# A decoder layer on one core: the output gate's projection woven into the cached-token attention instead of the mLSTM, and the sequences' states loaded ahead of their scores

## The chip, the cores and the metric

The kernel runs on one core of a Trainium2 chip. The metric is the device time of one execution in microseconds (us). The kernel before took 1005.29 us (median of 3 runs, 1005.04 to 1005.99). Engines are called PE (TensorE, with PEld for its weight loads), DVE (VectorE), ACT (ScalarE), POOL (GpSimd) and SP (SyncE, which here only issues DMAs).

## The reference

One layer of a hybrid decoder, for a prompt of 512 tokens and, beside it, 8 sequences with 4 new tokens each. The mixer has two heads groups side by side, an mLSTM and a differential attention (DA), both fed by the same normalised rows `h`:

```python
h = rms_norm(x, g_mix_pre)
z = h @ w_in
q, k, v, o = mLSTM columns of z          # 4 heads x 128 each
h_ml, C_new, n_new, m_new = mlstm_chunkwise(q, k, v, i_pre, logf, ml_C, ml_n, ml_m)
h_ml = rms_norm(h_ml, g_ml_head) * sigmoid(o)
dq, dk, dv = DA columns of z             # rotated
a = attend(dq, dk, dv, lam)              # prompt: causal; sequences: cache of 256 tokens + own 4
h_da = rms_norm(a, g_da_head) * (1 - lam_init)
x = x + rms_norm(concat(h_ml, h_da) @ w_out, g_mix_post)
x = x + rms_norm(cross attention into 256 memory tokens, g_mem_post)
x = x + rms_norm(conv_ffn(...), g_ffn_post)
```

For the 8 sequences the mLSTM starts from a given state: a matrix `C` of 128 x 128 for each sequence and head (32 matrices, 64 KB each), which is read, used for the output, updated and written back.

## The kernel before

All tokens are held as 5 row blocks: four of 128 prompt rows and one of the 32 rows of the sequences. Weights pass through a pool `W` of 4 slots (`wp`); each weight tile is loaded by SP, split on ACT (L142) and DVE (L143) into a high and a low part, and multiplied in three passes, so that a product of fp32 accuracy comes out of reduced-precision matmuls. `gemmA` makes row-major products, `gemmB` (L452) transposed ones; a `gemmB` step is one 128-column weight tile: 8 x 3 x 2 = 48 matmuls, half of them 256 and half 288 columns wide.

`F` is a queue of filler work: generators of projections, from which `F.run(n)` takes pieces worth about n us and emits them at that place of the program. The final order of each engine is made by a scheduler that keeps the dependences and moves ready work about. In the program's order the stretch that matters here is:

- the prompt's mLSTM, a pipeline over the 4 prompt blocks (`ml_own`, `ml_state`, `ml_rows`), with the DA projections as filler. The last filler is the output gate's projection `o`: `gemmB(hT, [ev_T(soT, h) ...])`, 4 steps, 192 matmuls, into `soT` (L617);
- the sequences' mLSTM scores (L788 to L927): scores, key weights `kS`, the normaliser `n` (in from HBM as `nrow`, out as `nrow`);
- the sequences' states, called the state stage below. `mls_load` brings the four matrices of one head and four sequences as a tile `Cs` (256 KB). `mls_update` reads them into the output (`mlsi`, L949: 16 matmuls for each group of four sequences), makes the update (`vz` on POOL, L936; `mlus` on PE, L952), adds it on DVE (L954, four instructions for each tile) and writes the tile back (L956). There are 8 tiles, two groups of 4 heads; the loads of the second group are issued as the first is worked off. All of these tiles come from a pool `T2` of 8 buffers;
- the cached-token attention, called the cache stage below: for each of the 8 sequences `dk_turn` transposes 256 cached keys (`tpk`, L1158, 8 transposes a sequence) and `dk_scores` makes the scores (`ssc`, L1164). Woven between them is the prompt's DA (`sda`, L1179 and L1180; `tpa`, L1195; `oda`, L1205). `out_gate` (sigmoid on ACT, L987; scale on POOL, L988; transposes `mlt`, L995) is put in from its fourth step on. The product with the cached values (`ops`, L1247) follows.

PE works its instructions in the order in which they stand, and so does SP with its DMAs: what waits holds up everything behind it.

Of the kernel before, what the change touches and what calls it, by code (L numbers as in the profile page):

```python
# [15 lines left out]
P = 128  # L16
# [6 lines left out]
H = 4  # L23
# [50 lines left out]
def kernel(ctx: ExitStack, tc: tile.TileContext, I, O):  # L74
# [23 lines left out]
    def S(shape, dt, name):  # L98
        return sp.tile(list(shape), dt, name=name, tag="S")
# [4 lines left out]
    def T2(shape, name, dt=F32):  # L104
        return t2p.tile(list(shape), dt, name=name, tag="T2")
# [4 lines left out]
    def at(name="at"):  # L110
        return psa.tile([P, 512], F32, name=name, tag="at")

    def mmp(name="mm"):
        return psm.tile([P, 512], F32, name=name, tag="mm")
# [8 lines left out]
    def v2(t, b):  # L123
        return t.rearrange("p (a b) -> p a b", b=b)
# [10 lines left out]
    dma = nc.sync.dma_start  # L135

    def f32(ap):
        return ap.bitcast(F32)
# [6 lines left out]
    def rows(b):  # L145
        return (b * P, P) if b < 4 else (SEQ, NS)
# [4 lines left out]
    def con(n, p=P):  # L151
        o, w = CONST_COLS[n]
        return cpk[:p, o:o + w]
# [173 lines left out]
    allb = [0, 1, 2, 3, 4]  # L327

    class Fill:
# [8 lines left out]
        def run(self, amount=1e9):  # L338
            while amount > 0 and self.q:
                try:  # L340
                    amount -= next(self.q[0])
                except StopIteration:
                    self.q.pop(0)

    F = Fill()
# [5 lines left out]
    def pipe(n, *stages):  # L351

        for t in range(n + len(stages) - 1):
            for s in reversed(range(len(stages))):
                if 0 <= t - s < n:
                    stages[s](t - s)
            yield

    def sample_mm(ps, xs, w, start, stop):


        for kk, x in enumerate(xs):
            n = x.shape[0]
            for e in range(2):
                g = NS * (2 * kk + e)
                mm(ps[g:g + NS, :256], lhsT=x, rhs=w[:n, kk, 256 * e:256 * e + 256], start=start, stop=stop)  # L366
# [7 lines left out]
    def gemmA(xt, nk, blocks, evac, block_major=False, before=None, mid=None, late=False):  # L374


        ps = {}

        def one(b, k, s):
            if b == 4:  # L380
                if k % 2 == 0:
                    sample_mm(ps[b], [xt.sam(k), xt.sam(k + 1)], s[1], k == 0, k == nk - 2)
                return
            s, kk = s[0], k % 2
            c0, n = rows(b)
            mm(ps[b], lhsT=xt.hi(k, c0, c0 + n), rhs=s[:, 0, kk, :], start=(k == 0), stop=False)  # L386
            mm(ps[b], lhsT=xt.hi(k, c0, c0 + n), rhs=s[:, 1, kk, :], start=False, stop=False)  # L387
            mm(ps[b], lhsT=xt.lo(k, c0, c0 + n), rhs=s[:, 0, kk, :], start=False, stop=(k == nk - 1))  # L388

        if block_major:  # L390
            slots = [W.get() for _ in range((nk + 1) // 2)]
            for b in blocks:
                if before:
                    before(b)
                ps[b] = mmp()
                for k in range(nk):
                    if k == MIDK and mid:
                        mid()
                    one(b, k, slots[k // 2])
                    if b == blocks[-1] and k % 2 == 1:  # L400
                        W.free()
                evac(b, ps[b])
                yield 5.1
        else:
            for b in blocks:
                ps[b] = mmp()
            behind = []
            for k in range(nk):
                if k % 2 == 0:
                    s = W.get()  # L410
                    if 4 in blocks:
                        behind.append((k, s))
                        if not late:
                            one(4, *behind.pop(0))
                for b in blocks:
                    if b < 4:
                        one(b, k, s)
                if k % 2 == 1:
                    if len(behind) > 1:
                        one(4, *behind.pop(0))  # L420
                    if not late or k > 1:
                        W.free()
                yield sum(0.64 if b < 4 else 0.43 for b in blocks)
            for k, s in behind:
                one(4, k, s)
                W.free()
            for b in blocks:
                evac(b, ps[b])
            yield 0

    def gemmB(xt, evacs, half_first=False):

        if half_first:
            slots = [W.get() for _ in evacs]
            for i, (c0, c1) in enumerate(HALF):
                for s, ev in zip(slots, evacs):
                    ps = mmp()[:, :c1 - c0]
                    for k in range(8):
                        for j, (l, x) in enumerate(((0, xt.hi), (0, xt.lo), (1, xt.hi))):
                            mm(ps, lhsT=s[:, l, k, :], rhs=x(k, c0, c1), start=(k == 0 and j == 0), stop=(k == 7 and j == 2))  # L440
                    if i == 1:
                        W.free()
                    ev(i, c0, c1, ps)
                    yield 2.6
            return
        for ev in evacs:
            s = W.get()
            ps = [mmp()[:, :c1 - c0] for c0, c1 in HALF]
            for k in range(8):
                for j, (l, x) in enumerate(((0, xt.hi), (0, xt.lo), (1, xt.hi))):  # L450
                    for i, (c0, c1) in enumerate(HALF):
                        mm(ps[i], lhsT=s[:, l, k, :], rhs=x(k, c0, c1), start=(k == 0 and j == 0), stop=(k == 7 and j == 2))  # L452
                if k % 2 == 1 and k < 7:
                    yield 1.36
            W.free()
            for i, (c0, c1) in enumerate(HALF):
                ev(i, c0, c1, ps[i])
            yield 1.36
# [79 lines left out]
    hT = XT("hT")  # L538
# [76 lines left out]
    def ev_T(dst, h):  # L615
        def ev(i, c0, c1, ps):
            nc.scalar.copy(out=dst[:, h, c0:c1], in_=ps)  # L617
        return ev
# [147 lines left out]
    def ev_dv(b, ps):  # L766
# [4 lines left out]
        else:  # L771
# [1 line left out]
            dma(out=O["s_dv"][0].rearrange("b t h d -> (b t) (h d)"), in_=dvS)  # L773

    soT = S([P, H, ROWS], F32, "soT")
    F.add(gemmA(hT, 8, allb, ev_dk), gemmA(hT, 8, allb, ev_dq), gemmA(hT, 8, allb, ev_dv),
          gemmB(hT, [ev_T(soT, h) for h in range(H)]))


    def ml_scores(b):  # L780

        c0, n = rows(b)

        eb = T2([P, H, n], "mlE", F32R)
        GTT(out=eb, in0=f32(E2[:, c0:c0 + n]).unsqueeze(1).broadcast_to([P, H, n]),
            in1=hsel.unsqueeze(2).broadcast_to([P, H, n]), op=MUL)
        dv = at("mld")[:, :H * n].rearrange("p (h n) -> p h n", n=n)
        mm(dv[:n], lhsT=ones_r[:, :n], rhs=eb, start=True, stop=False)  # L788
        mm(dv[:n], lhsT=identb[:n, :n], rhs=(maskTb if b < 4 else maskSb).unsqueeze(1).broadcast_to([n, H, n]),
           start=False, stop=True)  # L790
        dm = T2([n, H, n], "mlD")
        for h in range(H):
            ACT(out=dm[:, h, :], in_=dv[:n, h, :], func=AF.Exp, bias=gt4[:n, b, 0, h:h + 1])
        sv = v2(at("mls"), P)[:, :, :n]
        for h in range(H):
            mm(sv[:n, h, :], lhsT=kT[:, h, c0:c0 + n], rhs=qT[:, h, c0:c0 + n], start=True, stop=True)
        VTT(out=dm, in0=sv[:n], in1=dm, op=MUL)
        return dm
# [17 lines left out]
    mlh, Cs, dms, wks = {}, {}, {}, {}  # L816
# [65 lines left out]
    dma(out=O["p_ml_n"][0, 0], in_=nrow)  # L882


    sm_t = ml_scores(4)
    pk = at("mlks")
    for h in range(H):
# [39 lines left out]
    dma(out=O["s_ml_n"][0].rearrange("b h d -> (b h) d"), in_=nrow1)  # L927

    pi = at("mlsi")
    csts, vzs = {}, {}  # L930

    def mls_values(i):

        g, h = i // H, i % H
        vzs[i] = T2([P, 4, P], "vz", F32R)
        GTT(out=vzs[i], in0=f32(vS[:, h, :]).unsqueeze(1).broadcast_to([P, 4, P]),  # L936
            in1=con("selX")[:, 4 * g:4 * g + 4].unsqueeze(2).broadcast_to([P, 4, P]), op=MUL)

    def mls_load(g, h):
        csts[g, h] = T2([P, 4, P], "Cs")  # L940
        dma(out=csts[g, h], in_=I["state_ml_C"][0, 4 * g:4 * g + 4, h].rearrange("b d e -> d b e"))

    def mls_update(i):
        g, h = i // H, i % H
# [13 lines left out]
            mls_load(1, h)  # L958
        F.run(2.5)

    for h in range(H):
        mls_load(0, h)
    run(pipe(2 * H, mls_values, mls_update))
    pn = at("mlsn")
    for h in range(H):
# [248 lines left out]
    STT(out=cv, in0=con("cB"), scalar=nlam, in1=con("cA"), op0=MUL, op1=ADD)  # L1214

    W.nslots = 2
    prompt = pipe(4 * H, da_soft, lambda i: None, da_turn, da_av, da_end)
    sall = S([P, NB, 260], F32, "das")
    nm, su = small(NB, "snm"), small(NB, "ssu")
    for t, _ in enumerate(pipe(NB, dk_load, dk_turn, dk_scores)):  # L1220
        if t == 3:
            F.add(out_gate())
        F.run(2.5)
        next(prompt)
        F.run(2.5)
    aw, az = sample_softmax(sall, su, cv, con("selD"), "da")
    F.run(4)
    pz = Z("pz")[:, :NS]
# [554 lines left out]
```

## Time and profile before

| | |
|---|---|
| median of 3 runs | 1005.29 us |
| the profiled execution's own time | 1005.6 us |
| its span, first to last instruction | 1003.8 us |
| mean granted PE clock | 0.986 |
| PE busy | 975.0 us |
| DVE, ACT, POOL busy | 601.9, 388.4, 195.4 us |

The profile is of one execution. "Busy" of PE counts a matmul from its start to its modelled end; matmuls overlap, so PE may be busy without being at its peak. A row of the timeline gives the start in us from the span's beginning, the time that the merged instructions took together, the engine, the line of the code, the operation, what it writes and reads, how many instructions were merged (one matmul on plain fp32 counts twice), and in brackets the idle time before it with what ended it. A row of a table by windows gives, for each engine, the busy time in that window, then the granted PE clock (1.00 is full speed) and the share of time in which the DMA engines were busy.

### The profile page before, as it was taken

To read this page: it belongs to the slowest core of one execution; us is meant where nothing else is said; L and a number is where in the kernel's file an instruction comes from. 1 tells how busy PE (TensorE), PEld (TensorE's weight loads), DVE (VectorE), ACT (ScalarE), POOL (GpSimd) and SP (SyncE) were. 2 spreads that over 40 slices of the span, in tenths; PEclk is the share of its full clock that TensorE was granted. 3 is DMA by queue.
4 is the path that set the end of the run, shared out by engine and by line. 5 is a ranking of instruction groups with operands and counts; after the bars stand their busy time and mean duration, and the time that the engine had idled before them with its cause. 6 is when DMAs were issued, how large, how long until landed. Compare 5 with 4: busy or idle time off the path is not lost.

```text
span 1003.8 us, 17048 instructions
## 1 busy us (share of the span) xinstructions
PE 975.0 (97%) x6615; PEld 813.2 (81%) x6615; DVE 601.9 (60%) x1129; ACT 388.4 (39%) x746; POOL 195.4 (19%) x389
## 2 busy tenths in 40 slices
PE   8999999999799999999999999999999999999994
PEld 5899777889555778998757789979987997997983
DVE  5735324643686357634653587836857685675677
ACT  5654313334376348633442444242222222222232
POOL 6510000112332124400000264301101010110115
PEclk9999999999799999999999999999999999999998
DMA  8950224152534167764851673052142314214113
GB/s 276 302 156 20 65 84 129 43 182 60 175 115 145 40 210 255 252 206 157 325 199 42 194 236 106 26 146 86 45 116 75 96 46 126 87 44 135 34 47 110
DMA packets 120401, 130.26 MB, mean 130 GB/s; under 512 B 8423, under 2 KB 85832, under 8 KB 120320
## 3 DMA queue, kind: packets, MB, share of 16 engines
q1 hardware_dynamic: 114136, 125.69, 40.6%
q10 hardware_dynamic: 6184, 3.48, 1.2%
q8 instruction: 52, 0.85, 0.3%
q14 instruction: 29, 0.24, 0.1%
HBM read 112.22 MB, written 16.93 MB: 129 GB/s over the span
## 4 chain that ended last, share of the span: by engine, by line
PE 87%; DVE 5%; DMA 4%; issue 2%; ACT 2%; POOL 1%; ACTq 0%; SPq 0%; DVEq 0%; POOLq 0%
PE mm L452 30%; PE mm L440 7%; PE mm L386 6%; PE mm L388 6%; PE mm L387 6%; PE mm L1626 4%; PE mm L1628 4%; PE mm L1627 4%; PE mm L366 3%; PE sda L1179 2%; PE tpk L1384 1%; PE sca L1335 1%; PE cpo L1365 1%; PE ssc L1394 1%; PE oda L1205 1%
## 5 line engine op out<-in xcount | busy, mean ns | idle before, releaser
L142 ACT CAST wslot<-wst 128x1024 fp32r<-128x1024 f32 (+1 forms) x127 | 131.1, 1036 | 278.8 <-issue 81.2
L452 PE MATMUL mm<-fT,wslot 128*128 128x256 f32 (+1 forms) x1872 | 235.7, 288 | 0.0
L452 PEld LDWEIGHTS mm<-fT,wslot 128*128 128x128 f32 x1872 | 234.7, 188 | 0.7 <-issue 0.4
L143 DVE TENSOR_TENSOR wslot<-wst,wslot 128x1024 fp32r<-128x1024 f32 (+1 forms) x127 | 154.0, 1215 | 109.7 <-ACT wslot L142 109.7
L1626 PE MATMUL mm<-wslot,act 128*128 128x512 f32 (+1 forms) x176 | 70.7, 409 | 0.0
L1627 PE MATMUL mm<-wslot,act 128*128 128x512 f32 (+1 forms) x176 | 69.5, 395 | 0.0
L1628 PE MATMUL mm<-wslot,act 128*128 128x512 f32 (+1 forms) x176 | 69.0, 397 | 0.0
L1533 POOL COPY cvo<-u 128x2 f32<-128x2 f32 x43 | 16.1, 375 | 222.8 <-DVE u L1531 222.8
L386 PE MATMUL mm<-wslot,hT 128*128 128x512 f32 x128 | 51.9, 408 | 0.0
L452 PE MATMUL mm<-hT,wslot 128*128 128x288 f32 (+1 forms) x384 | 51.4, 290 | 0.0
L387 PE MATMUL mm<-wslot,hT 128*128 128x512 f32 x128 | 51.2, 400 | 0.0
L388 PE MATMUL mm<-wslot,hT 128*128 128x512 f32 x128 | 50.7, 397 | 0.0
L452 PEld LDWEIGHTS mm<-hT,wslot 128*128 128x128 f32 x384 | 48.9, 188 | 0.9 <-issue 0.8
L1626 PEld LDWEIGHTS mm<-wslot,act 128*128 128x128 f32 (+1 forms) x176 | 33.1, 189 | 17.7 <-issue 8.6
L1528 DVE TENSOR_TENSOR u<-mm,rsb 128x256 f32<-128x256 f32 x43 | 18.1, 423 | 44.2 <-PE mm L452 43.3
L1628 PEld LDWEIGHTS mm<-wslot,act 128*128 128x128 f32 (+1 forms) x176 | 33.0, 188 | 7.5
L1627 PEld LDWEIGHTS mm<-wslot,act 128*128 128x128 f32 (+1 forms) x176 | 33.1, 188 | 6.5
L1545 ACT ACTIVATE c<-c 128x560 f32<-128x560 f32 x21 | 14.1, 672 | 57.3 <-DVE c L1539 57.2
L1539 DVE SCALAR_TENSOR_TENSOR c<-u,cvT,c 128x560 f32<-128x560 f32 x43 | 34.3, 798 | 0.8
L1538 DVE SCALAR_TENSOR_TENSOR c<-u,cvT,c 128x560 f32<-128x560 f32 x43 | 34.1, 794 | 0.1
L1639 DVE TENSOR_TENSOR yp<-mm,yp 128x512 f32<-128x512 f32 x40 | 27.3, 689 | 9.5 <-PE mm L1628 9.4
L386 PEld LDWEIGHTS mm<-wslot,hT 128*128 128x128 f32 x128 | 24.0, 188 | 10.3 <-issue 5.8
(458 smaller groups left out, 1885.8 us busy)
## 6 DMA issues: line engine op xcount, KB each, us to landing
wst<-in_w_up_dram SPq DMA_DIRECT2D x42, 512.0 KB
wst<-in_w_in_dram SPq DMA_DIRECT2D x28, 512.0 KB
wst<-in_w_down_dram SPq DMA_DIRECT2D x20, 512.0 KB
wst<-in_cache_mem_k_dram SPq DMA_DIRECT2D x16, 512.0 KB
vt<-in_cache_mem_v_dram SPq DMA_DIRECT2D x8, 1024.0 KB
wst<-in_w_mk_dram SPq DMA_DIRECT2D x8, 512.0 KB
xb<-in_x_prompt_dram SPq DMA_DIRECT2D x8, 512.0 KB
wst<-in_cache_dk_dram SPq DMA_DIRECT2D x16, 256.0 KB
```

The source lines that it names most:

```text
L142: nc.scalar.copy(out=hi, in_=src)
L143: (eng or nc.vector).tensor_tensor(out=lo, in0=src, in1=f32(hi), op=SUB)
L386: mm(ps[b], lhsT=xt.hi(k, c0, c0 + n), rhs=s[:, 0, kk, :], start=(k == 0), stop=False)
L387: mm(ps[b], lhsT=xt.hi(k, c0, c0 + n), rhs=s[:, 1, kk, :], start=False, stop=False)
L388: mm(ps[b], lhsT=xt.lo(k, c0, c0 + n), rhs=s[:, 0, kk, :], start=False, stop=(k == nk - 1))
L440: mm(ps, lhsT=s[:, l, k, :], rhs=x(k, c0, c1), start=(k == 0 and j == 0), stop=(k == 7 and j == 2))
L452: mm(ps[i], lhsT=s[:, l, k, :], rhs=x(k, c0, c1), start=(k == 0 and j == 0), stop=(k == 7 and j == 2))
L1538: STT(out=c, in0=u[:, 1:EXT - 1], scalar=w[1], in1=c, op0=MUL, op1=ADD)
L1539: STT(out=c, in0=u[:, 0:EXT - 2], scalar=w[0], in1=c, op0=MUL, op1=ADD)
L1626: mm(ps, lhsT=t[:, 0, c0:c0 + P], rhs=s[:n, 0, i % 2, :], start=st, stop=False)
L1627: mm(ps, lhsT=t[:, 0, c0:c0 + P], rhs=s[:n, 1, i % 2, :], start=False, stop=False)
L1628: mm(ps, lhsT=t[:, 1, c0:c0 + P], rhs=s[:n, 0, i % 2, :], start=False, stop=en)
```

## The change

Three things are moved; no computation is added or left out.

1. The output gate's projection is no longer filler of the mLSTM. It is put into the filler queue just before the cache stage.
2. In the cache stage each step takes two pieces of about 1 us from the filler queue in place of two of about 2.5 us. `out_gate` still joins the queue at the fourth step, now behind the projection.
3. The loads of the first four state tiles are issued before the sequences' scores instead of after them.

```diff
     soT = S([P, H, ROWS], F32, "soT")
-    F.add(gemmA(hT, 8, allb, ev_dk), gemmA(hT, 8, allb, ev_dq), gemmA(hT, 8, allb, ev_dv),
-          gemmB(hT, [ev_T(soT, h) for h in range(H)]))
+    F.add(gemmA(hT, 8, allb, ev_dk), gemmA(hT, 8, allb, ev_dq), gemmA(hT, 8, allb, ev_dv))
...
+    csts, vzs = {}, {}
+
+    def mls_load(g, h):
+        csts[g, h] = T2([P, 4, P], "Cs")
+        dma(out=csts[g, h], in_=I["state_ml_C"][0, 4 * g:4 * g + 4, h].rearrange("b d e -> d b e"))
+
+    for h in range(H):
+        mls_load(0, h)
     sm_t = ml_scores(4)
...
     pi = at("mlsi")
-    csts, vzs = {}, {}
-
     def mls_values(i):
...
-    def mls_load(g, h):
-        csts[g, h] = T2([P, 4, P], "Cs")
-        dma(out=csts[g, h], in_=I["state_ml_C"][0, 4 * g:4 * g + 4, h].rearrange("b d e -> d b e"))
...
-    for h in range(H):
-        mls_load(0, h)
     run(pipe(2 * H, mls_values, mls_update))
...
     W.nslots = 2
+    F.run()
+    F.add(gemmB(hT, [ev_T(soT, h) for h in range(H)]))
     prompt = pipe(4 * H, da_soft, lambda i: None, da_turn, da_av, da_end)
     sall = S([P, NB, 260], F32, "das")
     nm, su = small(NB, "snm"), small(NB, "ssu")
     for t, _ in enumerate(pipe(NB, dk_load, dk_turn, dk_scores)):
         if t == 3:
             F.add(out_gate())
-        F.run(2.5)
+        F.run(1)
         next(prompt)
-        F.run(2.5)
+        F.run(1)
```

What the scheduler made of it is seen in three places. The first is SP's queue around the state tiles. `Cs<-in_state_ml_C` is the load of a tile, `out<-Cs` the write of an updated one, `nrow` the normaliser's rows. Before:

```order
L882 DMA out_dram<-nrow 4x128
L900 DMA nrow_2292<-in_state_ml_n_dram 32x128
L941 DMA Cs<-in_state_ml_C_dram 128x4x128
L927 DMA out_dram<-nrow_2321 32x128
L941 DMA Cs<-in_state_ml_C_dram 128x4x128 x5
L956 DMA out_dram<-Cs 128x4x128 x2
L941 DMA Cs<-in_state_ml_C_dram 128x4x128 x2
L956 DMA out_dram<-Cs 128x4x128 x5
```

After (line numbers move with the edit: L888 is the load, L957 the write, L934 the second `nrow` out):

```order
L888 DMA Cs<-in_state_ml_C_dram 128x4x128 x2
L881 DMA out_dram<-nrow 4x128
L888 DMA Cs<-in_state_ml_C_dram 128x4x128 x2
L907 DMA nrow_2182<-in_state_ml_n_dram 32x128
L888 DMA Cs<-in_state_ml_C_dram 128x4x128
L934 DMA out_dram<-nrow_2211 32x128
L888 DMA Cs<-in_state_ml_C_dram 128x4x128
L957 DMA out_dram<-Cs 128x4x128
L888 DMA Cs<-in_state_ml_C_dram 128x4x128
L957 DMA out_dram<-Cs 128x4x128 x2
L888 DMA Cs<-in_state_ml_C_dram 128x4x128
L957 DMA out_dram<-Cs 128x4x128 x4
```

Four loads now stand ahead of the `nrow` load. The sixth load stands behind the second `nrow` write, the seventh behind the first tile's write and the eighth behind the second tile's write; in the built program each of these three waits for the end of that write, whose buffer it takes over. Before, six loads stood ahead of every tile's write, and only the eighth waited for one.

The second place is PE in the state stage (`mlsi` reads the states, `mlus` makes an update). Before, a piece from its beginning:

```order
L949 MATMUL mlsi<-Cs,qzm 32x128
L452 MATMUL mm<-hT_255,wslot 128x288
L452 MATMUL mm<-hT_256,wslot 128x256
L452 MATMUL mm<-hT_256,wslot 128x288
L952 MATMUL mlus<-vz,kS 128x512
L452 MATMUL mm<-hT_255,wslot 128x256
L949 MATMUL mlsi<-Cs,qzm 32x128 x13
```

After, the whole stage with the first rows of the cache stage:

```order
L950 MATMUL mlsi<-Cs,qzm 32x128 x16
L953 MATMUL mlus<-vz,kS 128x512
L950 MATMUL mlsi<-Cs,qzm 32x128
L953 MATMUL mlus<-vz,kS 128x512
L950 MATMUL mlsi<-Cs,qzm 32x128
L953 MATMUL mlus<-vz,kS 128x512 x2
L950 MATMUL mlsi<-Cs,qzm 32x128
L953 MATMUL mlus<-vz,kS 128x512
L950 MATMUL mlsi<-Cs,qzm 32x128 x13
L953 MATMUL mlus<-vz,kS 128x512 x3
L965 MATMUL mlsn<-tb,mlD 32x128 x4
L1157 MATMUL tpk<-cpk,wst 128x128 x16
```

No `L452` stands in this stage any more. Of the projection's 192 matmuls the first step's 48 stay ahead of the sequences' scores, among the last rows of the prompt's mLSTM, together with 4 `sda` pairs of the DA that stood in the state stage before. The third place is PE in the cache stage. Before:

```order
L1180 MATMUL sda<-cb 128x128
L1158 MATMUL tpk<-cpk,wst 128x128 x8
L1164 MATMUL ssc<-kT,qz 32x260 x4
L995 MATMUL mlt<-cpk,mlh 128x128 x4
L1205 MATMUL oda<-dvN,aT 128x128
L1195 MATMUL tpa<-cpk,pda 128x128
```

After:

```order
L1179 MATMUL sda<-cb 128x128
L1163 MATMUL ssc<-kT,qz 32x260 x4
L1157 MATMUL tpk<-cpk,wst 128x128 x2
L452 MATMUL mm<-hT_255,wslot 128x256
L452 MATMUL mm<-hT_255,wslot 128x288
L452 MATMUL mm<-hT_256,wslot 128x256
L452 MATMUL mm<-hT_256,wslot 128x288
```

The other 144 matmuls of the projection stand here, in runs of 2 to 19 between the attention's groups, and the 17 `mlt` transposes have moved to the stage's end. Behind the cache stage PE's order is the same but for a few rows.

## The prediction

> **What bounds the kernel now.** I read the page's first and fourth parts, then a table by windows around the change, then the timelines and the chain of waits there.
>
> ```profile
> PE 975.0 (97%) x6615; PEld 813.2 (81%) x6615; DVE 601.9 (60%) x1129; ACT 388.4 (39%) x746; POOL 195.4 (19%) x389
> ...
> PE 87%; DVE 5%; DMA 4%; issue 2%; ACT 2%; POOL 1%; ACTq 0%; SPq 0%; DVEq 0%; POOLq 0%
> ```
>
> PE bounds the kernel: 97% busy, and 87% of the chain. Work that leaves a stretch in which PE is full shortens it, and work that enters one lengthens it; only where PE waits is there room. So the windows:
>
> ```profile
> 219.40:233.40 14.00, 14.00 (x117) 13.94 (x115) 6.54 (x21) 5.41 (x11) 4.63 (x7) 1.00 0.32 101
> ...
> 256.80:259.10 2.30, 0.44 (x3) 0.14 (x2) 2.12 (x10) 0.46 (x2) 1.04 (x1) 1.00 0.46 135
> 259.10:272.76 13.66, 10.34 (x64) 6.39 (x64) 7.44 (x27) 1.84 (x5) 3.99 (x6) 0.50 0.71 205
> 272.76:311.40 38.64, 36.62 (x251) 21.77 (x251) 30.72 (x82) 27.68 (x94) 13.87 (x16) 1.00 0.31 97
> ```
>
> The columns are PE, PEld, DVE, ACT, POOL, the granted clock and the DMA share. The mLSTM's end is full (14.00 of 14.00). The cache stage from 272.76 is nearly full (36.62 of 38.64: 2.0 idle). Between them lies a hole in the state stage, whose own lines are these, of PE and then of the chain:
>
> ```profile
> 246.84 0.41 PE L949 MATMUL mlsi<-Cs,qzm 128*32 128x128 f32 x2
> 250.79 1.06 PE L949 MATMUL mlsi<-Cs,qzm 128*32 128x128 f32 x26
> 258.43 0.41 PE L949 MATMUL mlsi<-Cs,qzm 128*32 128x128 f32 x2 [1.59 <-DMA Cs<-in_state_ml_C_dram]
> 260.62 1.92 PE L949 MATMUL mlsi<-Cs,qzm 128*32 128x128 f32 x26 [1.78 <-DMA Cs<-in_state_ml_C_dram]
> 267.67 3.64 PE L1158 MATMUL tpk<-cpk,wst 128*128 128x128 f32 x16 [0.38 <-DVE Cs L954]
> ```
>
> ```profile
> 253.14 4.40 DMA out_dram<-Cs
> 257.55 3.02 DMA Cs<-in_state_ml_C_dram
> ```
>
> The last tile's load waited for the end of a write (4.40), took 3.02, and PE began on it at 260.62. From there it was 7.05 us to the cache stage (267.67). The hole is the buffer chain: write ended, load, tail.
>
> **The change, part by part.** Up to the mLSTM's last update (219.4) nothing differs.
>
> *The lead-in.* Before, 96 projection matmuls stand between 219.4 and the scores' first matmul; now 48 and 4 `sda` pairs.
>
> ```profile
> 219.64 4.50 PE mm L452 x36
> 224.15 0.45 PE mli L857 x4
> ```
>
> ```profile
> 233.39 0.22 PE L788 MATMUL mld<-mlE,ones_r 128*32 128x128 f32 x1
> 253.20 0.49 PE L1179 MATMUL sda<-dkT,dqT 64*128 64x128 f32 x2
> 253.62 0.23 PE L1180 MATMUL sda<-cb 128*128 128x128 bf16 x1
> 253.78 0.48 PE L1179 MATMUL sda<-dkT,dqT 64*128 64x128 f32 x2
> ```
>
> One matmul is 4.50 / 36 = 0.125. Now: 48 x 0.125 = 6.0, four pairs at 253.78 - 253.20 = 0.58 make 2.3, four groups of `mli`/`mln` at 0.45 make 1.8: 219.4 + 10.1 = 229.5 (I say 229.6, for one transpose more). The scores start 3.8 earlier.
>
> *The scores.* No fill stands between them now, so a chain over ACT and DVE sets their length:
>
> ```profile
> 234.15 1.28 ACT L793 ACT_TABLE_LOAD   x1
> 235.45 0.79 ACT L793 ACTIVATE mlD<-mld,gt 32x32 f32<-32x32 f32 x4
> 237.55 0.66 ACT L987 ACTIVATE soT<-soT 128x544 f32<-128x544 f32 x1
> 238.11 0.60 ACT L890 CAST kS<-ta 32x512 fp32r<-32x512 f32 x1
> ```
>
> ```profile
> 238.75 1.52 DVE L893 TENSOR_TENSOR kS<-ta,kS 32x512 fp32r<-32x512 f32 x2 [2.20 <-ACT kS L890]
> ```
>
> ```profile
> 242.76 0.33 SPq L927 DMA_DIRECT2D out_dram<-nrow  x1
> ```
>
> ACT's order is now: exponentials, one table load, the first sigmoid, casts. From 229.6, two `mld` 0.4, exponentials 0.8, table load 1.3, sigmoid 0.65, cast 0.6: 233.35. Two subtractions 1.5: 234.85. From there to the `nrow` write it was 242.76 - 240.27 = 2.5 before, partly behind fill; I take 1.7 (an estimate). So the write is issued at 236.5, 6.3 earlier, and the first `mlsi` comes then too instead of at 246.84, PE waiting for most of the 4 us before it.
>
> *The buffer chain.* Four tiles land long before that, and the fifth. The sixth load takes a buffer that the `nrow` write holds. No row shows how long that write takes; the nearest is another small DMA, from its issue to the instruction that waited for it:
>
> ```profile
> L582 ACTq DMA_DIRECT2D lrow<-in_da_lambda_dram x1: 256/256/256, 52.1 to 52.1; - x1
> L585 DVE TENSOR_TENSOR lpr<-lrow x1: 279/279/279, 53.8 to 53.8; 1x128 f32<-1x128 f32 x1
> ```
>
> I take its 1.7, between the issue alone (0.33) and a tile's load (3.0): the sixth tile lands at 236.5 + 1.7 + 3.0 = 241.2. For the seventh, the first tile must be updated and written, and what that takes on PE depends on the clock. In the windows the clock fell at 259.10, when PE had had 0.44 of work in 2.30 us, and came back at 272.76, 5.1 after steady work began. Between the key products and the first `mlsi` PE now has some 5.5 us with these short groups in it:
>
> ```profile
> 237.62 0.24 PE L902 MATMUL nT<-cpk,nrow 32*128 32x32 f32 x1
> ...
> 238.11 1.05 PE L907 MATMUL mldn<-cpk,ta 32*128 32x8 f32 x8
> ...
> 240.90 0.23 PE L912 MATMUL mlg<-nT,qT 128*32 128x8 f32 x2
> ...
> 242.13 0.28 PE L924 MATMUL nTt<-cpk,nTn 128*32 128x128 f32 x1
> ```
>
> `mlg` fills 240.90 to 242.13, so they are 0.24 + 1.05 + 1.2 + 0.28 = 2.8, half of it. That is far more than 0.44 in 2.30, so I take full clock: 16 `mlsi`, which count twice, are 32 x 1.06 / 26 = 1.3 (half clock: 32 x 1.92 / 26 = 2.4).
>
> ```profile
> 248.69 0.39 PE L952 MATMUL mlus<-vz,kS 128*128 128x512 f32 x1
> 264.56 0.77 PE L952 MATMUL mlus<-vz,kS 128*128 128x512 f32 x1 [0.88 <-POOL vz L936]
> ```
>
> ```profile
> 250.78 2.11 DVE L954 SCALAR_TENSOR_TENSOR Cs<-Cs,dec,mlus 128x128 f32<-128x128 f32 x7 [1.31 <-PE mlus L952]
> 263.30 4.23 DVE L954 SCALAR_TENSOR_TENSOR Cs<-Cs,dec,mlus 128x128 f32<-128x128 f32 x16 [3.71 <-PE mlus L952]
> ```
>
> Then `mlus` 0.4 (0.77 at half clock) and four additions at 2.11 / 7 = 0.30: the first tile's write is issued at 236.5 + 1.3 + 0.4 + 1.2 = 239.4. Written at 243.8 (4.4), seventh tile landed at 246.8 (3.0). The second write stands behind the seventh load on SP, which holds the queue until 243.8; so it ends at 243.9 + 4.4 = 248.3, and the eighth tile lands at 251.3. Of the 7.05 from the last landing to the cache stage, 4.23 were 16 additions (0.264 each); with 12 to 15 left I take 6.4. `vz` on POOL runs beside this:
>
> ```profile
> 243.89 2.05 POOL L936 TENSOR_TENSOR vz<-vS,cpk 128x512 fp32r<-128x512 f32 x2
> ```
>
> 1.02 each, eight in 8.2; the last ones wait for the third and fourth writes' buffers (about 253), inside the tail. **The cache stage starts at 257.7, 10.0 earlier.** At half clock the first write would go 1.5 later, and so all of it: 259.2. The trace's fall after 2.3 us of near idleness leaves that open. The Trainium skill, "TensorE: Matmul & The Clock Gate", section "What's actually happening", has the clock halved after an idle window of about 3.4 us, which the new gaps don't reach; by it the sum stays at 257.7, but the windows' 2.3 is under it and no run here shows which share of work counts as idle.
>
> *The cache stage* took 267.67 to this row, 43.8:
>
> ```profile
> 311.44 0.86 PE L1247 MATMUL ops<-wst,daz 128*32 128x128 f32 x22
> ```
>
> Its start at half clock (5.1) stays: PE will have idled as before. 144 projection matmuls come in, 18.0 at 0.125; where a run of them is cut by short groups I allow some 5% more, 0.132 or 19.0 (an estimate), and take 18.5. The idle they can fill is the 2.0; I take 1.5, as the largest wait lies where a group already stands:
>
> ```profile
> PE tpk L1158 <- DVE kT L1159: 1.0, 1, 1.0
> ```
>
> New stalls: three sigmoids now fall between exponentials. Each changes ACT's table twice (2 x 1.28) and takes 0.66. Bounds are nothing (PE has projection to do meanwhile) and the whole 3 x 3.2 = 9.7; I take 1.0, near the lower end, since ACT is busy 27.68 of 38.64 and 9.7 fits in its idle 11. The order also runs the projection in PSUM buffers that nothing else there needs at that moment; I cost that at nothing, and in the third rival if it does. `mlt` transposes and POOL's scaling only change places within the stage. Sum: 43.8 + 18.5 - 1.5 + 1.0 = 61.8, so it ends at 257.7 + 61.8 = 319.5.
>
> **The sum**: 319.5 - 311.4 = +8.1. Behind it the order is the same and PE full, so the shift carries to the end: 1005.6 + 8.1 = 1013.7 for the profiled execution; the median is 0.3 under that one's time, so 1013.4. In short, before, 96 of the 144 moved matmuls (12 us) worked in time that PE would otherwise have spent in the scores' and state stage's waits; now they are paid in full.
>
> **The rivals.** Break-even is a cache stage that starts at 311.4 - 61.8 = 249.6.
>
> 1. *Early loads break the buffer chain* (faster). Then DVE's additions bound the state stage: first `mlus` at 237.8, 32 x 0.264 = 8.5, then `mlsn` and the last waits 1.0: start at 247.3, end at 309.1, 2.3 sooner: 1003.0. It wins where the stage starts before 249.6, 8.1 ahead of mine, so the two writes and two loads on the chain would have to cost less than half of the 14.8 I give them. For: four of eight loads are gone from the chain. Against: three stand behind writes.
> 2. *PE's busy time is overstated* (faster). Its weight loads are busy only 21.77 of 38.64 in the cache stage, against 13.94 of 14.00 in the fill's. If the rest, 16.9, is room, 18.5 - 16.9 = 1.6 is paid: 257.7 + 43.8 + 1.6 = 303.1, 8.3 sooner: 997.0. Against: the short groups follow each other without a gap that has a releaser, and their lengths repeat:
>
> ```profile
> 286.70 1.04 PE L1158 MATMUL tpk<-cpk,wst 128*128 128x128 f32 x8
> 287.68 0.70 PE L1179 MATMUL sda<-dkT,dqT 64*128 64x256 f32 x2
> ```
>
> Eight transposes in 0.98 are 0.12 each, the pace of the fill itself. The Trainium skill, "Perfetto Trace Analysis", section "Identifying the Most-Contended Engine", speaks for this rival: matmul busy time is called a poor measure, weight-load busy share a good one.
> 3. *ACT's table loads or PSUM bind the cache stage* (slower still). 9.7 instead of 1.0: +16.8, 1022.1. For: `sda`'s softmax passes through ACT and each next group needs its result. Against: the idle 11 us of ACT.
> 4. *It cancels*: nearer 249.6 by faster writes and by more of the idle filled: 1005.3.
>
> **How the numbers follow.** Forecast 0.77, rivals 0.06, 0.05, 0.09, 0.03. Its own range: down by writes at the load's price (2 x 1.4), no stalls (1.0), all idle filled (0.5), fill at 0.125 (0.5): 1008.6; up by a small write of 3.0 (1.3), half clock (1.5), nothing absorbed (1.5), 0.132 (0.5), two writes that share the DMA engines (1.0): 1019.2. To hold 8 in 10 it reaches to the fourth rival and most of the way to the third: 1004.5 to 1021. Within 0.2% (2 us), which a measurement of this kernel can't tell from none: 0.03; faster 0.11; slower 0.86.
>
> **What the profile would show.** Right: the scores' first matmul near 229.6; the `nrow` write near 236.5; loads six to eight each right after a write's end; `tpk` x16 near 258; full clock at the first `mlsi`; `ops` near 320; few table-load waits on PE. Wrong: a cache stage starting before 250; weight loads in it that rise with PE's total unchanged; or gaps of 2 us and more with ACT as releaser.

## The result, and the profile after

The changed kernel takes 1015.88 us (median of 5 runs, 1012.9 to 1016.82) against 1005.29. Taken over all runs it is 1.0097 times as long (95% interval 1.008 to 1.0115), which is 9.8 us; the two medians lie 10.6 apart, as these ratios are not quotients of medians. The forecast was 1013.4. One of the ten runs of no_sigmoid below took 1892.64 us, nearly twice its others, and its ratio leaves that run out. The profiled execution is the fastest of the five, 1012.9, with a span of 1011.1 against 1003.8.

First the scores and the state stage after: rows of PE's timeline, of SP's, and of the chain of waits.

```profile
230.53 0.22 PE L787 MATMUL mld<-mlE,ones_r 128*32 128x128 f32 x1
...
237.01 0.40 PE L931 MATMUL nTt<-cpk,nTn 128*32 128x128 f32 x1 [2.15 <-DVE nTn L929]
237.34 1.94 PE L950 MATMUL mlsi<-Cs,qzm 128*32 128x128 f32 x32
...
250.32 1.91 PE L950 MATMUL mlsi<-Cs,qzm 128*32 128x128 f32 x26 [2.31 <-DMA Cs<-in_state_ml_C_dram]
...
256.33 2.83 PE L1157 MATMUL tpk<-cpk,wst 128*128 128x128 f32 x16 [0.61 <-DVE Cs L955]
```

```profile
237.75 0.34 SPq L934 DMA_DIRECT2D out_dram<-nrow  x1
239.21 0.37 SPq L888 DMA_DIRECT2D Cs<-in_state_ml_C_dram  x1
241.19 0.38 SPq L957 DMA_DIRECT2D out_dram<-Cs  x1
```

```profile
241.19 2.30 DMA out_dram<-Cs
...
243.97 3.35 DMA out_dram<-Cs
...
247.33 2.95 DMA Cs<-in_state_ml_C_dram
```

The cache stage starts at 256.33 instead of 267.67, 11.3 us sooner. What holds it is still write, load, tail: the second write ends at 247.32, the eighth tile lands at 250.28, and PE, which waited 2.31 for it, needs 6.0 more.

Then the cache stage as one window, before and after (span, then busy PE, PEld, DVE, ACT, POOL, the clock, the DMA share):

```profile
267.67:311.44 43.77, 41.75 (x276) 25.48 (x277) 33.45 (x90) 29.29 (x98) 14.82 (x19) 0.94 0.39 120
```

```profile
256.33:320.02 63.69, 62.18 (x421) 44.28 (x421) 33.85 (x90) 41.79 (x114) 17.60 (x25) 0.92 0.27 83
```

It takes 63.7 instead of 43.8, so the 11.3 won before it are lost and 8.6 more. From `ops` on, 311.44 before and 320.02 after, the program takes 692.4 and 691.1: the loss lies ahead of `ops`.

A window's time can be taken apart with its own row. Idle is span less PE's busy time. Time lost to the clock is span times (1 - clock): at half clock half of the time is lost. The rest is PE's work at full clock. Before: 43.8 = 39.1 work + 2.6 clock + 2.0 idle. After: 63.7 = 57.1 + 5.1 + 1.5. The work rose by 18.0, which is 144 x 0.125. The clock's loss rose by 2.5, because of a second stretch at half clock that the kernel before doesn't have. In windows of 4 us of the changed kernel it stands at the stage's end:

```profile
308.00:312.00 4.00, 3.42 (x19) 1.80 (x22) 3.97 (x6) 2.42 (x7) 3.61 (x4) 0.98 0.00 0
312.00:316.00 4.00, 3.28 (x22) 1.51 (x18) 3.82 (x11) 2.69 (x14) 2.47 (x3) 0.50 0.00 0
316.00:320.00 4.00, 4.00 (x14) 2.08 (x12) 0.56 (x1) 0.76 (x3) 0.00 (x0) 0.67 0.00 0
```

### The profile page after: what moved, and what is told of

Same layout as the page of the kernel before. It is cut to its first block, busy times and chain, and to the rows that moved or that the text cites. A ratio compares the mean times of both kernels' runs of the same rounds, so it can differ in the third digit from the quotient of the medians.

```text
span 1011.1 us, 17069 instructions
## 1 busy us (share of the span) xinstructions
PE 976.6 (97%) x6615; PEld 813.4 (80%) x6615; DVE 603.9 (60%) x1129; ACT 393.3 (39%) x750; POOL 196.7 (19%) x389
## 4 chain that ended last, share of the span: by engine, by line
PE 84%; DVE 6%; DMA 4%; issue 2%; ACT 2%; POOL 1%; SPq 0%; DVEq 0%; POOLq 0%; ACTq 0%
PE mm L452 30%; PE mm L386 7%; PE mm L387 6%; PE mm L388 6%; PE mm L440 5%; PE mm L1627 4%; PE mm L1629 4%; PE mm L1628 4%; PE mm L366 3%; PE sda L1178 2%; DMA xb<-x_d 2%; PE tpk L1385 1%; PE sca L1336 1%; PE cpo L1366 1%; PE ssc L1395 1%
## 5 line engine op out<-in xcount | busy, mean ns | idle before, releaser
L452 PE MATMUL mm<-fT,wslot 128*128 128x256 f32 (+1 forms) x1872 | 235.8, 288 | 0.0
L452 PEld LDWEIGHTS mm<-fT,wslot 128*128 128x128 f32 x1872 | 234.8, 188 | 0.7 <-issue 0.4
L452 PE MATMUL mm<-hT,wslot 128*128 128x288 f32 (+1 forms) x384 | 54.4, 294 | 0.0
L452 PEld LDWEIGHTS mm<-hT,wslot 128*128 128x128 f32 x384 | 49.7, 189 | 2.1 <-issue 1.7
L1546 ACT ACTIVATE c<-c 128x560 f32<-128x560 f32 x21 | 14.1, 673 | 57.3 <-DVE c L1540 57.2
L1540 DVE SCALAR_TENSOR_TENSOR c<-u,cvT,c 128x560 f32<-128x560 f32 x43 | 34.3, 797 | 0.8
```

The costliest lines, as they stand in the source:

```text
L1540: STT(out=c, in0=u[:, 0:EXT - 2], scalar=w[0], in1=c, op0=MUL, op1=ADD)
```

## The experiments

Times are medians; a ratio is to the kernel before, run beside it on the same chip, over all runs. Stage lengths come from one profiled execution, whose own time lies between 4 us under its kernel's median (vz_elsewhere) and 2 us over it (gate_late). "State" is from the scores' first matmul (`mld`) to `tpk` x16, "cache" from there to `ops`. "Work" is PE's work at full clock in the cache stage, taken from its window as above.

| kernel | time, us | ratio (95%) | state | cache | work | clock | idle |
|---|---|---|---|---|---|---|---|
| before | 1005.29 | | 34.3 | 43.8 | 39.1 | 2.6 | 2.0 |
| changed | 1015.88 | 1.0097 (1.008 to 1.0115) | 25.8 | 63.7 | 57.1 | 5.1 | 1.5 |
| loads_only | 1003.93 | 0.9985 (0.9971 to 0.9998) | 30.8 | 43.1 | 39.3 | 1.7 | 2.0 |
| projection_only | 1017.91 | 1.014 (1.011 to 1.017) | 29.0 | 65.4 | 57.5 | 5.2 | 2.7 |
| short_projection | 1009.58 | 1.0041 (1.0026 to 1.0056) | 25.7 | 58.1 | 45.1 | 7.6 | 5.4 |
| vz_elsewhere | 1011.57 | 1.0073 (1.0047 to 1.01) | 20.6 | 63.4 | 57.8 | 3.2 | 2.4 |
| no_sigmoid | 1010.52 | 1.0044 (1.0025 to 1.0063) | 24.4 | 60.6 | 57.3 | 1.8 | 1.5 |
| gate_late | 1025.84 | 1.0189 (1.0143 to 1.0235) | 25.9 | 71.1 | 59.9 | 9.2 | 2.0 |
| loads_vz | 995.57 | 0.9894 (0.9849 to 0.9939) | 23.9 | 40.5 | 39.3 | 0.0 | 1.2 |
| state_vz | 994.78 | 0.9891 (0.9842 to 0.9941) | 27.7 | 40.4 | 39.2 | 0.0 | 1.2 |
| one_sigmoid | 1015.04 | 1.010 (1.0066 to 1.0134) | 23.9 | 67.2 | 56.2 | 6.7 | 4.3 |
| late_fill | 1021.25 | 1.0144 (1.0118 to 1.017) | 24.1 | 64.1 | 60.7 | 1.3 | 2.1 |
| vz_only | 1001.09 | 0.995 (0.9933 to 0.9966) | 30.7 | 42.0 | 39.1 | 1.7 | 1.2 |

The clock is given to 0.01, so work and clock are good to 0.3. In gate_late the gate's transposes end inside the stage behind more of the DA's, in late_fill a part of the fill lies beyond it, so their work isn't the same set.

"State" begins at `mld`, and loads_only and loads_vz have 113 projection matmuls between the mLSTM's last update and `mld`, where the kernel before has 96 and the changed kernel 48. Counted from that last update to the cache stage, which holds lead-in, scores and states, the stretch is 48.3 us before, 46.9 in loads_only, 44.7 in vz_only, 40.0 in loads_vz, 39.7 in state_vz, 39.4 in projection_only, 36.2 in the changed kernel and 31.0 in vz_elsewhere.

**The parts apart.** loads_only is the kernel before with part 3 of the change, projection_only the changed kernel without it:

```diff
+    for h in range(H):
+        mls_load(0, h)
     sm_t = ml_scores(4)
...
-    for h in range(H):
-        mls_load(0, h)
     run(pipe(2 * H, mls_values, mls_update))
```

> The third part of the change alone: the first four state tiles are loaded ahead of the scores, the projection stays filler of the mLSTM, pieces of 2.5 in the cache stage. Theory A (the change loses because 144 projection matmuls are moved out of time in which PE waits into a stage in which it is full, and wins back a part by the shorter load-write-load chain): the chain alone is shortened, the cache stage starts some 3 us sooner than before (near 264.5), time about 1002 (999 to 1004.5). Theory B (the loads' place is worth nothing because three loads still wait for writes): 1005, no change. Theory C (early loads disturb the mLSTM's end): slower than 1007.

> The first two parts alone: the projection is filler of the cache stage, the state tiles are loaded where they were. Theory A: the chain of loads and writes starts with the earlier nrow write but has all eight loads behind it, so the cache stage starts near 260 and pays the same 18 us of projection: about 1018 (1016 to 1021), 2 to 4 above the changed kernel. Theory B: equal to the changed kernel within 1 us. If the projection itself were cheap in the cache stage (theory D: PE's busy time hides room), this would be no slower than before, 1005.

Both times came out as theory A has it, the first only just: 0.15% faster, its interval ending at 0.9998, and 1.4% slower. One start did not: projection_only's cache stage was expected near 260 and began at 256.36, as early as the changed kernel's, because its mLSTM ended at 217.00 in that execution and the changed kernel's at 220.12. So lengths are compared here. The early loads shorten the stretch up to the cache stage by 1.4 us without the projection moved (48.3 to 46.9) and by 3.2 with it (39.4 to 36.2); the state stage's 34.3 to 30.8 says too much, since 17 more matmuls (2.1 us) stand ahead of it in loads_only. The moved projection lengthens the cache stage about as much with the early loads (43.1 to 63.7) as without (43.8 to 65.4). At its old place it was not free: without it the stretch up to the cache stage is 8.9 us shorter (48.3 to 39.4), about half of its 18.0 of work. So the loss is the projection's, and the loads win 2 us of it back by the medians, 4 by the ratios.

**Is each projection matmul paid?** In steps 2 to 4 only one of three products is made, with everything else in its place:

```diff
+            terms = ((0, xt.hi), (0, xt.lo), (1, xt.hi))[:1 if short and e else 3]
...
-                for j, (l, x) in enumerate(((0, xt.hi), (0, xt.lo), (1, xt.hi))):
+                for j, (l, x) in enumerate(terms):
```

> The changed kernel with one of the three products in steps 2 to 4 of the projection, so that 48 instead of 144 of its matmuls stand in the cache stage; the output gate's values are less exact. Theory A (every matmul in the cache stage is paid): 96 x 0.125 = 12 us less than the changed kernel, about 1004 (1003 to 1006). Theory D (PE has room there): at most 3 us less, 1013 to 1016. Theory E (the stage is bound by softmax and table loads on ACT): about 6 us less, since what is taken off PE shows up as waiting.

1009.6 is 6.3 under the changed kernel, the size of theory E, yet the window shows theory A's law and where the rest went:

```profile
254.08:312.18 58.10, 52.68 (x324) 34.12 (x325) 33.27 (x90) 41.34 (x114) 17.53 (x25) 0.87 0.29 90
```

```profile
PE sda L1180 <- ACT pda L1184: 3.6, 3, 1.9
PE spt L1037 <- ACT spc L1034: 0.9, 1, 0.9
PE spa L1032 <- DVE csz L1023: 0.8, 1, 0.8
PE tpk L1159 <- DVE Cs L957: 0.4, 1, 0.4
```

Work fell by 57.1 - 45.1 = 12.0, the full 96 x 0.125. In its place came 3.9 of idle, mostly `sda` waiting for the softmax on ACT, and 2.5 more lost to the clock, which fell after the longest of these waits. That wait, up to 286.46, has a table load of ACT just ahead of the softmax that ends it:

```profile
284.55 1.28 ACT L1184 ACT_TABLE_LOAD   x1
```

The projection had been covering ACT there; what one takes off PE is partly given back as waits.

**ACT's tables and the gate.** Three edits, of no_sigmoid, one_sigmoid and gate_late in this order: an exponential in place of the sigmoid takes the table loads away; one sigmoid over all four heads leaves a single pair of them in place of four; and the gate can be queued behind the loop:

```diff
-            ACT(out=soT[:, h], in_=soT[:, h], func=AF.Sigmoid)
+            ACT(out=soT[:, h], in_=soT[:, h], func=AF.Exp)
```

```diff
-        for h in range(H):
-            ACT(out=soT[:, h], in_=soT[:, h], func=AF.Sigmoid)
+        ACT(out=soT, in_=soT, func=AF.Sigmoid)
+        for h in range(H):
```

```diff
-        if t == 3:
-            F.add(out_gate())
...
     aw, az = sample_softmax(sall, su, cv, con("selD"), "da")
+    F.add(out_gate())
```

> The changed kernel with an exponential in place of the output gate's sigmoid, so that ACT changes no table in the cache stage; the gate's values are others. Theory A (the projection covers the table loads; PE's waits in the stage were 1.5 us in all): 0 to 2 us less than the changed kernel, the cache stage 62 to 63.7. Theory E (softmax behind the table loads sets the stage's pace): 5 to 9 us less, the stage near 56.

> The changed kernel with one sigmoid instruction over all four heads, after the whole projection, in place of one for each head: two table loads in the cache stage in place of six more. Theory A with J (table loads cost through short PE waits at the stage's end, and those through the clock): the single pair falls near 297 to 301, where the fill has run out, so the waits there stay, and the time is within 2 us of the changed kernel, either way. Theory E (table loads themselves bind): 3 to 6 us less.

> The changed kernel with out_gate put into the filler queue after the cache stage's loop instead of at its fourth step: no gate transposes, products and casts stand at the stage's end any more. Theory G (the gate's work on DVE and ACT there delays the softmax of the sequences, PE waits a little at the stage's end and then works at half clock, about 3.5 us lost at 312 to 319 of the changed kernel): no half clock after 300, 3 to 5 us less than the changed kernel, 1011 to 1013. Theory H (that half clock comes by itself in this stage): within 1 us of the changed kernel, the half-clock stretch still there.

no_sigmoid is about 5 us faster than the changed kernel, but neither theory has it right. Its stage is 3.1 shorter, and idle is 1.5 as before: ACT, busy 34.02 instead of 41.79, gave PE no waits back. All of the 3.1 is the clock, which doesn't fall a second time in this profile. Ahead of the stage, 1.4 us are chance: the scores began at 229.1 for 230.5 because the mLSTM ended that much sooner. But the state stage is shorter too (24.4 for 25.8), and most of that is a table load's own price. In the changed kernel the first sigmoid's load stands in the scores' chain, where nothing covers it:

```profile
231.96 1.28 ACT L986 ACT_TABLE_LOAD   x1
```

no_sigmoid has none there, and its `nrow` write goes out 6.08 us after the first `mld` instead of 7.22 (5.25 in one_sigmoid, where the whole sigmoid is gone from there). These are no_sigmoid's windows at the cache stage's end; PE had less work in one of them (2.68 of 4.00) than in the changed kernel's at that place, and the clock stayed:

```profile
304.00:308.00 4.00, 3.85 (x16) 1.79 (x16) 3.96 (x10) 2.79 (x8) 2.99 (x3) 1.00 0.00 0
308.00:312.00 4.00, 2.68 (x29) 1.66 (x28) 3.49 (x11) 2.70 (x14) 2.47 (x3) 1.00 0.00 0
```

one_sigmoid is level with the changed kernel, as theory A with J expected: its state stage is 1.9 shorter, but its single pair of loads makes two long waits (2.3 and 1.5) where no fill is left, and half clock from 307 to 317. gate_late was meant to relieve the stage's end and is 10 us slower, so theory G falls in the form I gave it. The clock falls behind one wait, `sda` for ACT, 1.5 us, right behind a table load (1.28 from 299.58) and at a place where the gate's transposes had been PE's only cover:

```profile
PE sda L1178 <- ACT pda L1182: 1.5, 1, 1.5
```

```profile
300.00:304.00 4.00, 2.53 (x15) 0.94 (x14) 1.79 (x5) 3.44 (x11) 2.65 (x2) 1.00 0.00 0
304.00:308.00 4.00, 4.00 (x14) 2.31 (x11) 2.50 (x9) 1.86 (x8) 0.00 (x0) 0.52 0.02 6
308.00:312.00 4.00, 4.00 (x12) 1.99 (x10) 1.13 (x5) 1.60 (x5) 0.00 (x0) 0.50 0.00 0
```

Half clock for 14 us follows, with PE fully busy in the first three windows of 4 us, and another such stretch of 17 us from 338. In the cache stage table loads thus cost little by their own length and several us through the clock, where nothing covers them.

**Where the fill ends.** late_fill takes three pieces of the queue where the changed kernel takes four (by the loop's ten turns 15 and 20, not 12 and 16 as the expectation counts them); after_again is the changed kernel beside it.

```diff
-        F.run(1)
+        F.run(0.5)
         next(prompt)
-        F.run(1)
+        if t % 2:
+            F.run(1)
```

> The changed kernel with fewer pieces taken at each step of the cache stage (12 instead of 16), so that the projection reaches to the stage's end and a part beyond it. Theory J (PE waits at the end because the fill has run out, and the clock falls for it): no half-clock stretch in the cache stage, 2 to 4 us less than the changed kernel if no wait of the kind comes later. Theory H (the clock's second fall has nothing to do with the fill): unchanged within 1 us, or more, since the gate comes later still.

> The changed kernel itself, beside the next two on the same chip. 1013 to 1017, some 1.0% over the kernel before. Theory J (the half-clock stretch at the cache stage's end is entered after a few short waits and left at a time that varies from run to run): its own runs spread over 3 us or more, and the stretch in the profile has another length than the 7 us of the first one.

after_again took 1015.81 us, 1.0098 times before (1.0068 to 1.0128), and its profile has the same stretch at 312 to 319. That doesn't refute theory J, though: by luck the moments at which the clock can change (see below) lie within 0.13 us of the first profile's, so the repetition doesn't show what happens where they lie elsewhere. Its runs spread over 4.4 us, but those of the kernel before beside it did too (1004.87 to 1009.26). In late_fill the stage's end is at full clock, as J has it, and yet the time is 1021, not 2 to 4 us less than the changed kernel: the remaining fill and the gate now come in the next stage, where PE waits for longer and the clock falls there:

```profile
300.00:318.00 18.00, 16.73 (x107) 9.93 (x106) 13.36 (x32) 14.51 (x42) 4.87 (x5) 1.00 0.01 1
318.00:332.00 14.00, 11.19 (x169) 7.43 (x168) 7.26 (x12) 5.45 (x13) 4.39 (x6) 1.00 0.75 241
332.00:345.00 13.00, 12.50 (x29) 6.01 (x28) 8.69 (x16) 8.16 (x20) 2.91 (x3) 0.51 0.22 76
```

**The buffer chain.** `vz` goes to another pool, so that eight buffers of T2 are left for the state tiles:

```diff
-        vzs[i] = T2([P, 4, P], "vz", F32R)
+        vzs[i] = zp.tile([P, 4, P], F32R, name="vz", tag="Z")
```

vz_elsewhere is this on the changed kernel, vz_only on the kernel before, loads_vz on loads_only. state_vz is it on the changed kernel with the projection queued just ahead of the state stage:

```diff
+    F.add(gemmB(hT, [ev_T(soT, h) for h in range(H)]))
     run(pipe(2 * H, mls_values, mls_update))
...
-    F.run()
-    F.add(gemmB(hT, [ev_T(soT, h) for h in range(H)]))
     prompt = pipe(4 * H, da_soft, lambda i: None, da_turn, da_av, da_end)
```

> The changed kernel with the eight vz tiles taken from the pool Z instead of T2, so that only one load of a state tile still waits for a tile's write instead of two with one more behind the nrow write. Theory A (buffer chain load-write-load sets the state stage's length): the cache stage starts about 3 to 5 us sooner, near 252, the time is about 1012 (1010 to 1014). Theory F (the state stage is bound by its updates on PE, DVE and POOL one after the other): it starts at most 1 us sooner, the time stays at 1015 to 1016.

> The kernel before with nothing but the vz tiles taken from the pool Z, the loads and the projection where they were. Theory K (early loads and free buffers each shorten the state stage, and the half clock goes once PE's waits there are short enough): the stage is shortened by part of what loads_vz gained, the cache stage starts 3 to 6 us sooner than before, 998 to 1002, with some half clock left. Theory L (the free buffers alone are worth it, the early loads nothing): as loads_vz, 994 to 997, and no half clock. Theory M (without early loads the freed buffers are worth nothing, since the loads still stand behind the nrow write): 1004 to 1006.

> Early loads alone, as in loads_only, with the vz tiles taken from Z, so that one load instead of three stands in the buffer chain; the projection is where it was before. Theory A (the chain sets the state stage's length, the cache stage keeps its 43): the cache stage starts 4 to 6 us sooner than in loads_only, the time is 997 to 1000. Theory F (without fill the updates bind): no more than 1 us under loads_only.

> The changed kernel with the projection put into the filler queue just ahead of the state stage, in pieces of 2.5 there and 1 in the cache stage, and vz taken from Z. Theory A (a projection matmul costs nothing where PE waits and 0.125 where it is full): nearly all of the projection is worked off before the cache stage, which takes 43 to 45 again; 997 to 1002. If the projection in the state stage delayed the updates as much as it fills (theory I), the cache stage would start some 10 us later than in vz_elsewhere and the time would be 1004 to 1008.

The chain set the state stage: on the changed kernel it is 5.2 shorter with one write in it (theory A), the time 4.3 lower by the medians, 2.4 by the ratios. On the kernel before, the buffers alone give 0.5% (theory K), the early loads alone 0.15%, and both together 1.06%, more than the sum, though the interval (0.61 to 1.51%) just reaches it. The stretch up to the cache stage says the same: 48.3 before, 44.7 and 46.9 by one of the two, 40.0 by both. With both, no wait of PE there reaches 1 us, the clock doesn't fall there at all, and the cache stage, with the same instructions but for a few rows in another order, takes 40.5 instead of 43.8. Theory A had it take 43 or more in loads_vz and state_vz; so both kernels beat what was expected of them (997 or more). PE's waits from 219 to 262 in loads_vz, and the cache stage's window:

```profile
PE mlus L954 <- DVE Cs L956: 0.8, 1, 0.8
PE mlsn L966 <- DVE Cs L956: 0.8, 1, 0.8
PE tpk L1158 <- ACT numS L968: 0.4, 1, 0.4
```

```profile
258.65:299.16 40.51, 39.33 (x277) 23.99 (x277) 32.33 (x94) 28.94 (x98) 14.84 (x19) 1.00 0.41 131
```

state_vz reaches the same by the other way: it puts the projection back to where PE waits, and beats the kernel before by 1.1%. Beside vz_elsewhere, from which it differs in nothing but the projection's place, it is the plainest test of that place: the stretch up to the cache stage is 8.7 longer (31.0 to 39.7), the cache stage 23.0 shorter (63.4 to 40.4), and the clock, at half from 232.79 to 253.27 in vz_elsewhere, doesn't fall. loads_vz and state_vz are the fastest kernels here, 10 us under before, and not told apart.

## Why the prediction was right

It was right in sign and size, +8.1 forecast and 9.8 measured (+8.6 at `ops` and +7.3 at the end between the two profiles), and in its main mechanism: projection matmuls that had in part worked in time in which PE waits anyway are paid in full in a stage where PE is full. The part is smaller than it said: 12 us of the moved work were to have been covered by waits, but without the 144 matmuls (18.0) the stretch up to the cache stage is 8.9 shorter in projection_only, so 9.1 were (an estimate from two profiles). That `ops` came at 320.0, forecast 319.5, is also luck: the cache stage began 1.4 too early and took 1.9 too long. By its steps:

- *Lead-in.* The scores began at 230.53, forecast 229.6; 0.7 of that is the mLSTM, which ended at 220.1 instead of 219.4 in this execution.
- *Scores.* The `nrow` write went out at 237.75, forecast 236.5. From the scores' first matmul to it are 7.2 us, forecast 6.9: the chain over ACT and DVE is what I made it.
- *Buffer chain.* The start at 256.33 was forecast as 257.7, but out of two errors. I took full clock for the first tile; it was half (32 passes in 1.94, as 26 in 1.92 before). I had compared with 0.44 of work in 2.30 us, but the last 3.41 us ahead of the fall held 1.41 of work before and 1.56 in the changed kernel, so that comparison did not speak for full clock. The first write went out at 241.19 instead of 239.4. And I gave both writes the 4.4 us of the last write before; they took 2.30 and 3.35. Loads (2.95 against 3.0) and tail (6.0 against 6.4) fit.
- *Cache stage.* 63.7, forecast 61.8. Fill 18.0 (forecast 18.5). The term that was mis-sized is "new stalls, 1.0": PE's idle did not rise, but a second half-clock stretch lost 3.4 at the end, while the first one cost about 1 less than before. I had looked at ACT's idle share and not at where the fill would run out.
- *The rivals.* The second rival (room inside PE's busy time) is refuted: weight-load busy time rose by 18.8 with PE's 20.4, and taking 96 matmuls out took 12.0 of work out. Here PE's busy time, corrected for the clock, was the better measure of what a stage can take; the Trainium skill, "Perfetto Trace Analysis", section "Identifying the Most-Contended Engine", would have pointed the other way. The first rival's mechanism is real, but even with one write less the cache stage began at 249.76, about the break-even. That profiled execution then reached `ops` 1.7 us later than before (313.14 against 311.44), because the cache stage took 63.4 and not 61.8; its kernel's four runs lie 0.7% over before. The third rival's 9.7 did not come as table loads: no_sigmoid bounds them at 3.1 in the stage, all of it clock. PSUM was not tested by itself, but PE's idle of 1.5 in the stage leaves no room for such waits.

When the clock can change, the traces show. In each of them all its changes lie a whole number of 3.41 us apart. In the changed kernel it is at half from 236.73 to 240.14, 243.55 to 253.79, 257.20 to 260.62 and 311.82 to 318.64: one, three, one and two times 3.41. The Trainium skill, "TensorE: Matmul & The Clock Gate", section "What's actually happening", speaks of a freely running window of that length; here the trace agrees. What stays open is which window makes the clock fall. These are the windows ahead of a fall in the changed kernel and in gate_late, and one of no_sigmoid after which the clock stayed:

```profile
308.41:311.82 3.41, 2.83 (x13) 1.21 (x12) 3.38 (x6) 2.00 (x6) 3.20 (x4) 1.00 0.00 0
300.73:304.15 3.42, 2.65 (x15) 1.02 (x15) 1.94 (x5) 2.80 (x11) 1.92 (x2) 1.00 0.02 5
307.91:311.32 3.41, 2.09 (x24) 1.11 (x24) 3.34 (x11) 2.56 (x14) 2.47 (x3) 1.00 0.00 0
```

It fell after 2.83 and 2.65 us of busy PE and stayed after 2.09, so PE's busy time in the profile is not the measure. That PE's waits alone cause the fall at the stage's end is not shown.

## What to carry to other kernels

A filler's worth is that of its place: the same 144 matmuls cost 8.9 us where PE waits for a part of the time and 18.0 where it is full, so before moving fill compare PE's idle in both stretches. Take a window apart into work, idle and clock; a wait of 1.5 us without cover cost up to 7 us more through the clock, and a stage may be lengthened by a wait ahead of it. Where loads wait for writes of the same pool, free buffers and earlier loads helped more together here than each alone.

## What was not expected of the hardware

- With the same instructions but for a few rows in another order, the cache stage took 43.8 at a mean clock of 0.94 and 40.5 at 1.00: of these 3.3 us, 2.6 are a stretch at half clock that begins before the stage, at 259.11.
- The clock changes only at whole multiples of 3.41 us, and half clock outlasts its cause: after one wait of 1.5 us in gate_late it stayed for 13.65 us, four times 3.41, with PE busy all of the first three.
- The write of a 256 KB state tile took 2.30 and 3.35 us in the changed kernel, 4.40 before and 4.20 in loads_vz.
